# Sums of weight blocks in the retention stage: made by accumulating transfers on GpSimd's queue instead of VectorE, with other signs and another order of the seven block products

## The chip, the cores and the metric

The kernel runs on one core of a Trainium2 chip. The metric is the device time of one execution in microseconds (us), the median of several runs; lower is better. The profile is of one execution, taken by the hardware profiler; its engines are PE (TensorE matmul), PEld (TensorE weight load), DVE (VectorE), ACT (ScalarE), POOL (GpSimd) and SP (SyncE, which here issues the transfers).

## What is computed

The reference is a two-layer decoder trunk over 1024 tokens of width 1024. Layer 0 is retention with four heads; layer 1 is stick-breaking attention. The change lies wholly in layer 0:

```python
u = rms_norm(h, ret_norm_pre[i])
proj = u @ ret_w_in[i]
q, k, v, g = jnp.split(proj, [RET_QK_WIDTH, 2 * RET_QK_WIDTH, 2 * RET_QK_WIDTH + RET_WIDTH], axis=-1)
...
o = retention_chunkwise(q, k, v)
...
o = merge_heads(o).astype(h.dtype) * jax.nn.silu(g)
y = o @ ret_w_out[i]
```

For one head, v is the normed input times a block of 1024 x 512 of the weights, and the gate g is the same input times another such block.

## The kernel before, in words

**Halves and phases.** The tokens are worked in two halves of 512 (t = 0 and 1). For each half, layer 0 goes through its four heads (u = 0 to 3), and a head has three main stages on TensorE: the projection to q and k (`qk`), the projections to v and g (`vg`), and the output projection of the head before (`out`). Of the eight stages for v and g, the first (t = 0, u = 0) is made by plain products (`first_v`, `first_g`); the other seven go through `vg` (lines 453 to 547), which the change rewrites. They start at 147, 251, 338, 461, 567, 675 and 760 us of the profiled span. The second layer runs from about 810 us on and isn't touched.

**Three matmuls for one product.** Every operand is split into a high and a low part (`split`, lines 259 to 266): ScalarE writes the high part (line 262), VectorE subtracts it from the value and so gets the low part (line 263). `mm3` (lines 107 to 112) adds up three matmuls, high x high, high x low and low x high.

**Seven products for eight.** `vg` takes v and g of one head together as one product of 2 x 2 blocks: rows of two blocks of 256 tokens, an inner dimension of two halves of 512, columns v and g. It is done in Winograd's form with seven block products, numbered 1 to 7, for eight. Each is 24 matmuls of 512 columns, in four chunks (`chunk`, line 514); its weights come in two units of 128 x 1024 (i = 0, 1), each of two pieces of 128 x 512 (256 KB). The products 1, 2 and 4 take a block of the weights as it is. Products 5, 6, 3 and 7 take sums and differences of blocks. Product 5 needs the sum of both gate blocks; 6 is that less a block of v; 3 and 7 are made from the one for 6. The running sum is kept in the tile S, one of 128 x 1024 for each i.

**Who makes the weights now.** `left` (lines 460 to 493) loads each piece into a wraw tile (six buffers, line 470), and for products 5, 6, 3 and 7 VectorE adds or subtracts (lines 480, 483, 486, 489); then `split` writes the unit of the matmul's operand, whl (three buffers). The sums of the inputs' blocks on the other side are made once for each half by `sums` (lines 312 to 325).

**What becomes of the products.** The order is 1, 2, 5, 6, 3, 7, 4. PSUM has eight banks, two each with the tags ma, mb, z and o. Product 1 goes to ma and 6 and 7 add to the same banks; 5 goes to mb and 3 adds to it; 2 goes to o; 4 takes mb anew. At the end of products 1, 5, 6 and 7 ScalarE copies the two banks (line 504); VectorE adds copies and banks (line 508) to get v (`vput`, lines 425 to 427, which splits it) and g (`gput`, lines 429 to 432: a sigmoid on ScalarE, a product on VectorE).

**What else lies in the stage.** `begin` (lines 645 to 648) puts the first two or three steps of the retention, `mix` (lines 584 to 643), into the last eight chunks; each takes a bank with tag o (line 607) and sends three small operations to GpSimd (lines 621 to 623), on which ScalarE waits at line 635. In some stages there are also the scores (`scores`, line 567, with a GpSimd select at line 575) or, in the stage from 567 us on, steps that finish the first half (`a_post`: line 693 on VectorE, 694 and 703 on GpSimd, 702 on ScalarE).

**What sets the order.** The source gives an order of steps (`merge`, line 209), which is a priority. The framework makes from it, when the kernel is built, a fixed order for each engine and each queue: an instruction whose inputs and buffers its plan has ready goes into an idle place, ahead of steps that stand before it in the source. On the chip every queue then runs strictly in that order. All transfers of this kernel are issued by SP.

Of the kernel before, what the change touches and what calls it, by code (L numbers as in the profile page):

```python
# [11 lines left out]
F32R = mybir.dt.float32r  # L12
# [19 lines left out]
def trunk(ctx, tc, xT, wts, gains, trig, ident_in, cols, out):  # L32
# [256 lines left out]
    def a_prep(t):  # L289

        X = Ctx()
        X.xh, X.T, X.raw = [None] * 8, [None] * 4, [None] * 4
        X.cos, X.sin = S("tab", [512]), S("tab", [512])

        def tables():
            dma(X.cos[:], trig[0, :, HT * t:HT * t + HT])
            dma(X.sin[:], trig[1, :, HT * t:HT * t + HT])

        tags = ["A"] * 5 + ["AT"] * 3

        def norm(k):
            i, c = k % 4, k // 4
            if t and c == 0:
                X.raw[i] = a_load(t, i, "S")
                if i == 3:
                    tables()
            src = X.raw[i][:, 512 * c:512 * c + 512]
            V.scalar_tensor_tensor(src, src, gcol(G_PRE, k), X.row[:], ALU.mult, ALU.mult)
            x = X.xh[k] = hl("xh")
            split((x[:, 0, :], x[:, 1, :]), src)  # L310

        def sums(i):

            raw = X.raw[i]
            q = [raw[:, 256 * n:256 * n + 256] for n in range(4)]
            X.T[i] = []
            a, b = S("f2", [2, 256]), S("f2", [2, 256])
            V.tensor_tensor(a[:, 0], q[0], q[1], ALU.subtract)
            V.tensor_tensor(a[:, 1], q[2], a[:, 0], ALU.subtract)
            V.tensor_tensor(b[:, 0], q[2], q[0], ALU.subtract)  # L320
            V.tensor_tensor(b[:, 1], q[3], a[:, 1], ALU.subtract)
            for f in (a, b):
                x = S(tags.pop(0), [2, 2, 256], F32R)
                split((x[:, :, 0, :], x[:, :, 1, :]), f[:])
                X.T[i] += [x[:, 0], x[:, 1]]

        if t:
            return X, [f for i in range(4) for f in (lambda i=i: norm(i), lambda i=i: norm(4 + i), lambda i=i: sums(i))]


        first = Ctx()
        first.xh = [None] * 8

        def load(k):
            i, c = k % 4, k // 4
            if c == 0:
                X.raw[i] = S("S" if i < 2 else "ko", [1024])
            src = X.raw[i][:, 512 * c:512 * c + 512]
            dma(src, xT[128 * k:128 * k + 128, 0:HT])
            if k == 0:  # L340
                first.o = S("oT", [4, 2, 512], F32R)
            if k == 4:
                first.o = S("qk", [4, 2, 512], F32R)
            x = first.xh[k] = first.o[:, k % 4]
            split((x[:, 0, :], x[:, 1, :]), src, gcol(G_PRE, k))
            if k == 0:
                first.acc = S("acc", [512])
                A_.activation(first.acc[:], src, AF.Square)
# [60 lines left out]
    class AHead:  # L409
# [16 lines left out]
            x = self.v[tb] = hl("v")  # L426
            split((x[:, 0, :], x[:, 1, :]), src, c)

        def gput(self, tb, src):
            g = self.sg[tb] = S("sg", [512])  # L430
            A_.activation(g[:], src, AF.Sigmoid)
            V.tensor_tensor(g[:], src, g[:], ALU.mult)
# [20 lines left out]
        def vg(self):  # L453


            X, base, h = self.X, self.base, self.h
            self.v, self.sg = [None] * 4, [None] * 4
            box = {"S": [None, None]}

            def left(n, i):  # L460

                w = S("whl", [2, 1024], F32R)
                if n == 5:
                    box["S"][i] = S("S", [1024])
                for c in range(2):
                    cl = slice(512 * c, 512 * c + 512)

                    def load(which, kk):
                        raw = S("wraw", [512])
                        dma(raw[:], wts[base + 4 + 4 * which + kk, :, cl])  # L470
                        return raw[:]

                    s = box["S"][i][:, cl] if box["S"][i] else None
                    if n == 1:
                        src = load(0, i)
                    elif n == 2:
                        src = load(0, 2 + i)
                    elif n == 5:
                        a, b, src = load(1, i), load(1, 2 + i), s
                        V.tensor_tensor(src, a, b, ALU.add)  # L480
                    elif n == 6:
                        a, src = load(0, i), s
                        V.tensor_tensor(src, src, a, ALU.subtract)
                    elif n == 3:
                        src = load(0, 2 + i)
                        V.tensor_tensor(src, src, s, ALU.subtract)
                    elif n == 7:
                        a, src = load(1, 2 + i), s
                        V.tensor_tensor(src, a, src, ALU.subtract)
                    else:  # L490
                        src = load(1, 2 + i)
                    split((w[:, 0, cl], w[:, 1, cl]), src)
                return w

            def right(n, kt, tb):
                tl = slice(128 * tb, 128 * tb + 128)
                if n in (1, 2, 3):
                    x, o = X.xh[kt + (0 if n == 1 else 4)], 0 if n == 3 else 256
                    return [x[:, l, o + 128 * tb:o + 128 * tb + 128] for l in range(2)]
                return [X.T[kt][{5: 0, 6: 1, 7: 2, 4: 3}[n]][:, l, tl] for l in range(2)]  # L500

            def copy(p):
                c = S("f2", [512])
                A_.activation(c[:], p[:], AF.Copy)
                return c

            def plus(c, p):
                V.tensor_tensor(c[:], p[:], c[:], ALU.add)
                return c[:]

            order = [(n, i) for n in (1, 2, 5, 6, 3, 7, 4) for i in range(2)]
            get = ahead(14, lambda at: left(*order[at]))

            def chunk(n, i, kk):
                if kk == 0:
                    at = order.index((n, i))
                    get(at)
                    get(at + 1)
                    box["w"] = get(at)
                    if i == 0:  # L520
# [12 lines left out]
                for tb, p in enumerate(banks):  # L533
                    if n in (1, 5, 6, 7):
                        box[n, tb] = copy(p)
                    if n in (1, 5, 6):
                        pass
                    elif n == 2:
                        self.vput(2 + tb, plus(box[1, tb], p), cc[:, 4 * h + 2 + tb:4 * h + 3 + tb])
                    elif n == 3:  # L540
                        self.vput(tb, plus(box[6, tb], p), cc[:, 4 * h + tb:4 * h + tb + 1])
                    elif n == 7:
# [4 lines left out]
            return Chunks([lambda n=n, i=i, kk=kk: chunk(n, i, kk) for n, i in order for kk in range(2)], lambda: get(0))  # L547
# [612 lines left out]
```

## Time and profile before

| what | value |
|---|---|
| runs: median of 3 (lowest, highest) | 1784.63 us (1782.44 to 1787.44) |
| span of the profiled execution | 1779.2 us |
| instructions | 23669 |
| HBM read, written | 233.93 MB, 56.62 MB |
| busy: PE, DVE, ACT, POOL | 1732.0, 1198.6, 815.1, 290.2 us |

The span goes from the first to the last instruction that the profile has; the median lies 5.4 us above it. A time of an execution includes the start and the end, which the span leaves out. The profile gives the profiled execution no time besides its span, so differences are worked out on the span and added to the median. The page of the profile lists busy times, the span in 40 slices and the costliest groups; the trace behind it can be asked for single stretches.

### The profile page before, as it was taken

The page shows a single profiled execution, that of the slowest core. Times are in us where ns is not written, and L with a number is a line of the kernel's source. Part 1 is how long each engine was busy: PE and PEld are TensorE (multiplying, and loading weights), DVE is VectorE, ACT ScalarE, POOL GpSimd, SP SyncE. Part 2 cuts the span into 40 slices and gives each one's busy share as a digit, 9 for nine tenths or more (in the row PEclk, how much of TensorE's full clock was granted, in tenths as well). Part 3 has the DMA queues.
Part 4 walks back from the last instruction along what each step waited for, and adds up shares of the span by engine and source line. Part 5 has one row for each costly group of instructions (what it writes and reads, how often), then busy time and mean ns, then how long its engine had stood idle before and what let it go on. Part 6 is the DMA issues. An engine that isn't in the chain of part 4 may idle for free.

```text
span 1779.2 us, 23669 instructions
## 1 busy us (share of the span) xinstructions
PE 1732.0 (97%) x8132; PEld 1432.3 (81%) x8132; DVE 1198.6 (67%) x1947; ACT 815.1 (46%) x1526; POOL 290.2 (16%) x377
## 2 busy tenths in 40 slices
PE   8999999999999999999999999999999999999997
PEld 6888788777788788877887888888778888888886
DVE  7756767789766868697485455556677456656675
ACT  6435545455445535364344343444445434444441
POOL 0210412232304320111130100000200010000003
PEclk9999999999999999999999999999999999999999
DMA  5225465557445646275664526345644433522243
GB/s 192 84 101 195 153 236 173 193 179 271 168 143 189 226 144 233 97 258 187 230 222 159 194 95 204 117 151 173 221 135 158 140 131 103 179 94 99 95 137 113
DMA packets 152553, 292.14 MB, mean 164 GB/s; under 512 B 17136, under 2 KB 19312, under 8 KB 152432
## 3 DMA queue, kind: packets, MB, share of 16 engines
q1 hardware_dynamic: 152432, 290.63, 48.2%
q8 instruction: 64, 1.05, 0.2%
q14 instruction: 57, 0.47, 0.1%
HBM read 233.93 MB, written 56.62 MB: 163 GB/s over the span
## 4 chain that ended last, share of the span: by engine, by line
PE 42%; issue 27%; DVE 16%; DMA 7%; POOL 4%; ACT 3%; SPq 1%; POOLq 0%; DVEq 0%; ACTq 0%
PE pma L111 6%; PE pmb L110 6%; PE pmb L111 6%; PE pmb L112 6%; PE pma L112 6%; PE pma L110 6%; DVE whl L263 3%; DMA wraw<-in_wts_dram 3%; PE po L111 2%; PE po L112 2%; PE po L110 2%; DVE sgn L838 1%; POOL small L622 1%; DMA y<-f 1%; DMA S<-in_xT_dram 1%
## 5 line engine op out<-in xcount | busy, mean ns | idle before, releaser
L263 DVE TENSOR_TENSOR whl<-wraw,whl 128x512 fp32r<-128x512 f32 x312 | 220.5, 735 | 67.8 <-ACT whl L262 67.2
L266 DVE SCALAR_TENSOR_TENSOR whl<-wraw,gn,whl 128x256 fp32r<-128x256 f32 (+1 forms) x256 | 153.5, 643 | 127.7 <-ACT whl L265 124.9
L262 ACT ACTIVATE whl<-wraw 128x512 fp32r<-128x512 f32 x312 | 183.5, 624 | 111.5 <-PE pmb L112 52.4
L265 ACT ACTIVATE whl<-wraw,gn 128x256 fp32r<-128x256 f32 (+1 forms) x256 | 143.1, 612 | 166.3 <-PE pmb L112 135.7
L110 PE MATMUL pmb<-xh,whl 128*128 128x512 f32 x384 | 153.1, 399 | 2.8 <-DVE sg L806 2.6
L110 PE MATMUL pma<-xh,whl 128*128 128x512 f32 x384 | 153.3, 399 | 1.2 <-DVE v L263 0.7
L112 PE MATMUL pmb<-xh,whl 128*128 128x512 f32 x384 | 150.3, 391 | 0.0
L112 PE MATMUL pma<-xh,whl 128*128 128x512 f32 x384 | 150.2, 391 | 0.0
L111 PE MATMUL pma<-xh,whl 128*128 128x512 f32 x384 | 149.8, 390 | 0.0
L111 PE MATMUL pmb<-xh,whl 128*128 128x512 f32 x384 | 149.7, 390 | 0.0
L836 POOL TENSOR_SCALAR_AFFINE_SELECT sgn<-sgn 128x128 f32<-128x128 f32 x64 | 24.8, 387 | 692.0 <-ACT sgn L831 580.1
L838 DVE TENSOR_TENSOR_SCAN sgn<-sgn 128x128 f32<-128x128 f32 (+3 forms) x64 | 89.1, 1393 | 45.0 <-POOL sgn L836 45.0
L263 DVE TENSOR_TENSOR AT<-pz,AT 128x512 fp32r<-128x512 f32 (+1 forms) x96 | 53.0, 553 | 72.3 <-ACT AT L262 71.9
L262 ACT ACTIVATE AT<-pz 128x512 fp32r<-128x512 f32 (+1 forms) x96 | 46.7, 487 | 111.5 <-PE pz L868 108.9
L110 PEld LDWEIGHTS pmb<-xh,whl 128*128 128x128 f32 x384 | 72.2, 188 | 18.5 <-DVE sg L806 5.3
L112 PEld LDWEIGHTS pmb<-xh,whl 128*128 128x128 f32 x384 | 72.1, 188 | 15.8
L112 PEld LDWEIGHTS pma<-xh,whl 128*128 128x128 f32 x384 | 72.1, 188 | 15.6
L110 PEld LDWEIGHTS pma<-xh,whl 128*128 128x128 f32 x384 | 72.2, 188 | 15.0 <-DVE v L263 1.1
L111 PEld LDWEIGHTS pmb<-xh,whl 128*128 128x128 f32 x384 | 72.2, 188 | 13.4
L111 PEld LDWEIGHTS pma<-xh,whl 128*128 128x128 f32 x384 | 72.3, 188 | 13.0
L110 PE MATMUL pma<-oT,whl 128*128 128x512 f32 x208 | 82.2, 395 | 0.5 <-DVE small L619 0.5
L111 PE MATMUL pma<-oT,whl 128*128 128x512 f32 x208 | 81.4, 392 | 1.2 <-DVE oT L263 1.2
(321 smaller groups left out, 4507.4 us busy)
## 6 DMA issues: line engine op xcount, KB each, us to landing
wraw<-in_wts_dram SPq DMA_DIRECT2D x624, 256.0 KB, 3.2
y<-f SPq DMA_DIRECT2D x120, 256.0 KB, 3.2
f<-y SPq DMA_DIRECT2D x88, 256.0 KB, 3.8
v<-v SPq DMA_DIRECT2D x16, 512.0 KB, 3.3
vo<-v SPq DMA_DIRECT2D x32, 256.0 KB, 2.9
A<-h SPq DMA_DIRECT2D x12, 512.0 KB, 4.3
st<-ko SPq DMA_DIRECT2D x8, 512.0 KB, 3.9
sg<-in_xT_dram SPq DMA_DIRECT2D x16, 256.0 KB, 2.9
```

Source lines behind the costliest of these rows:

```text
L110: MM(p, lh, rh, start=start, stop=False, **kw)
L111: MM(p, lh, rl, start=False, stop=False, **kw)
L112: MM(p, ll, rh, start=False, stop=stop, **kw)
L262: A_.activation(dst[0], src, AF.Copy)
L263: V.tensor_tensor(dst[1], src, f32(dst[0]), ALU.subtract)
L265: A_.activation(dst[0], src, AF.Copy, scale=scale)
L266: V.scalar_tensor_tensor(dst[1], src, scale, f32(dst[0]), ALU.mult, ALU.subtract)
L622: G.tensor_tensor(r[:], r[:], mhalf[:, 0:1], ALU.pow)
L836: G.affine_select(n[:, dg], n[:, dg], [[-1, 128]], ALU.is_gt, 1.0, base=0, channel_multiplier=1)
L838: V.tensor_tensor_scan(n[:, :W][:, ::-1], n[:, :W][:, ::-1], n[:, :W][:, ::-1], 1.0, ALU.mult, ALU.bypass)
```

## The change

Who adds the weight blocks is changed, and with it the signs and the order.

- A new step `fetch` makes the pieces: a plain transfer from SP brings the first block, and for products 5, 6, 3 and 7 a transfer issued by GpSimd adds a second block to what lies in the tile (`accum_op=ALU.add`). S is summed up in place: gate blocks for 5, a block of v more for 6, the other block of v for 3. Product 7 gets a sum of its own in wraw tiles.
- `left` only splits. The fetch of a unit stands three units ahead of its use in the source, and `begin` fetches three units before the stage starts.
- Since transfers only add, signs move: to the sums of the inputs (`sums`) and to the gate, where `gput` gets the negative of g and multiplies by -1.
- The order is 1, 5, 2, 6, 4, 3, 7. Product 4 uses the banks o, 3 and 7 still add to mb and ma. The copies of products 5 and 4 go into the gate tiles sg, and at the end of product 7 four additions read its two banks, each twice.

```diff
-            V.tensor_tensor(a[:, 0], q[0], q[1], ALU.subtract)
-            V.tensor_tensor(a[:, 1], q[2], a[:, 0], ALU.subtract)
+            V.tensor_tensor(a[:, 0], q[1], q[0], ALU.subtract)
             V.tensor_tensor(b[:, 0], q[2], q[0], ALU.subtract)
-            V.tensor_tensor(b[:, 1], q[3], a[:, 1], ALU.subtract)
+            V.scalar_tensor_tensor(a[:, 1], b[:, 0], -1.0, q[1], ALU.mult, ALU.subtract)
+            V.scalar_tensor_tensor(b[:, 1], a[:, 1], -1.0, q[3], ALU.mult, ALU.subtract)
...
-        def gput(self, tb, src):
+        def gput(self, tb, src, sign=1.0):
+            if sign < 0:
+                f = S("f2", [512])
+                A_.activation(f[:], src, AF.Sigmoid, scale=-1.0)
+                V.scalar_tensor_tensor(src, src, -1.0, f[:], ALU.mult, ALU.mult)
+                return
...
-            def left(n, i):
+            def fetch(n, i):
+                part = {1: (0, i), 2: (0, 2 + i), 4: (1, 2 + i), 5: (1, i), 7: (0, i)}
+                more = {5: (1, 2 + i), 6: (0, i), 3: (0, 2 + i), 7: (1, i)}
                 if n == 5:
                     box["S"][i] = S("S", [1024])
+                src = [box["S"][i][:, 512 * c:512 * c + 512] if n in (5, 6, 3) else S("wraw", [512])[:] for c in range(2)]
+                for c, p in enumerate(src):
+                    if n in part:
+                        which, kk = part[n]
+                        dma(p, wts[base + 4 + 4 * which + kk, :, 512 * c:512 * c + 512])
+                for c, p in enumerate(src):
+                    if n in more:
+                        which, kk = more[n]
+                        G.dma_start(p, wts[base + 4 + 4 * which + kk, :, 512 * c:512 * c + 512], accum_op=ALU.add)
+                return src
+
+            def left(at):
+                src = raw(at)
+                w = S("whl", [2, 1024], F32R)
                 for c in range(2):
...
-                    split((w[:, 0, cl], w[:, 1, cl]), src)
+                    split((w[:, 0, cl], w[:, 1, cl]), src[c])
                 return w
...
-            order = [(n, i) for n in (1, 2, 5, 6, 3, 7, 4) for i in range(2)]
-            get = ahead(14, lambda at: left(*order[at]))
+            order = [(n, i) for n in (1, 5, 2, 6, 4, 3, 7) for i in range(2)]
+            raw = ahead(14, lambda at: fetch(*order[at]))
+            get = ahead(14, left)
...
                     get(at)
                     get(at + 1)
+                    raw(at + 3)
...
-                        first = {1: "ma", 2: "o", 5: "mb", 4: "mb"}.get(n)
+                        first = {1: "ma", 2: "o", 5: "mb", 4: "o"}.get(n)
...
-                    if n in (1, 5, 6, 7):
+                    if n in (1, 6):
                         box[n, tb] = copy(p)
-                    if n in (1, 5, 6):
-                        pass
+                    elif n in (5, 4):
+                        self.sg[tb if n == 5 else 2 + tb] = copy(p, "sg")
...
-                    elif n == 7:
-                        self.gput(tb, plus(box[5, tb], p))
                     else:
-                        self.gput(2 + tb, plus(box[7, tb], p))
+                        plus(self.sg[tb], p)
+                        plus(self.sg[2 + tb], p)
+                if n == 7:
+                    for tb in range(4):
+                        self.gput(tb, self.sg[tb][:], -1.0)
...
+            def begin():
+                for at in range(3):
+                    raw(at)
+                get(0)
```

More of the change, by code (lines that the diff above doesn't have):

```diff
@@ L458, in vg @@
             box = {"S": [None, None]}
-            def left(n, i):
-                w = S("whl", [2, 1024], F32R)
+            def fetch(n, i):
+                part = {1: (0, i), 2: (0, 2 + i), 4: (1, 2 + i), 5: (1, i), 7: (0, i)}
+                more = {5: (1, 2 + i), 6: (0, i), 3: (0, 2 + i), 7: (1, i)}
                 if n == 5:
                     box["S"][i] = S("S", [1024])
+                src = [box["S"][i][:, 512 * c:512 * c + 512] if n in (5, 6, 3) else S("wraw", [512])[:] for c in range(2)]
[8 more added lines that the diff above has]
+                return src
@@ L465, in left @@
+            def left(at):
+                src = raw(at)
+                w = S("whl", [2, 1024], F32R)
                 for c in range(2):
                     cl = slice(512 * c, 512 * c + 512)
[L468 to L486, printed above, removed]
-                    elif n == 7:
[L488 to L491, printed above, removed]
@@ L500, in right, with copy @@
                 return [X.T[kt][{5: 0, 6: 1, 7: 2, 4: 3}[n]][:, l, tl] for l in range(2)]
-            def copy(p):
-                c = S("f2", [512])
+            def copy(p, tag="f2"):
+                c = S(tag, [512])
                 A_.activation(c[:], p[:], AF.Copy)
@@ L541, in chunk @@
                         self.vput(tb, plus(box[6, tb], p), cc[:, 4 * h + tb:4 * h + tb + 1])
-                    elif n == 7:
-                        self.gput(tb, plus(box[5, tb], p))
-                    else:
-                        self.gput(2 + tb, plus(box[7, tb], p))
-            return Chunks([lambda n=n, i=i, kk=kk: chunk(n, i, kk) for n, i in order for kk in range(2)], lambda: get(0))
+                    else:
+                        plus(self.sg[tb], p)
[7 more added lines that the diff above has]
+                get(0)
+            return Chunks([lambda n=n, i=i, kk=kk: chunk(n, i, kk) for n, i in order for kk in range(2)], begin)
         def out(self, y_d, acc=None, tags=None):
```

## The prediction

> **What bounds the kernel now.** First the page's head and the busy times, then the queues.
>
> ```profile
> span 1779.2 us, 23669 instructions
> ...
> PE 1732.0 (97%) x8132; PEld 1432.3 (81%) x8132; DVE 1198.6 (67%) x1947; ACT 815.1 (46%) x1526; POOL 290.2 (16%) x377
> ...
> q1 hardware_dynamic: 152432, 290.63, 48.2%
> ```
>
> TensorE is busy in 97% of the span, but its rows overlap, so the share doesn't say how near it is to its best. The timeline does: rows of the stage that starts at 147 us, the first matmul of product 1 and the first of product 2, 24 matmuls later.
>
> ```profile
> 147.04 0.39 PE L110 MATMUL pma<-whl,xh 128*128 128x512 f32 x1
> 147.27 0.39 PE L111 MATMUL pma<-whl,xh 128*128 128x512 f32 x1
> ...
> 152.48 0.39 PE L110 MATMUL po<-whl,xh 128*128 128x512 f32 x1
> ```
>
> Each row lasts 0.39 us, yet they start every (152.48 - 147.04) / 24 = 0.227 us. That is the pace to compare with; a unit of weights (12 matmuls) is worth 2.72 us, a product 5.44 us. Third, the busy times by stretch, one for each of the seven v and g stages that the change rewrites.
>
> ```profile
> core 0: us, PE busy (x) PEld busy (x) DVE busy (x) ACT busy (x) POOL busy (x), PEclk, DMA share, GB/s
> 147.00:187.20 40.20, 40.20 (x179) 33.26 (x179) 35.54 (x60) 24.89 (x44) 2.88 (x3) 1.00 0.60 201
> 251.40:292.30 40.90, 40.48 (x179) 33.16 (x179) 36.48 (x62) 24.15 (x43) 2.88 (x3) 1.00 0.58 198
> 338.30:386.60 48.30, 47.19 (x217) 38.49 (x216) 39.77 (x68) 29.02 (x53) 14.14 (x7) 0.97 0.66 218
> 460.80:509.20 48.40, 47.48 (x215) 38.81 (x214) 46.89 (x75) 30.22 (x55) 14.90 (x11) 1.00 0.51 175
> 567.40:618.50 51.10, 46.28 (x191) 36.20 (x189) 43.22 (x66) 27.63 (x49) 15.88 (x13) 0.97 0.72 244
> 675.30:719.20 43.90, 43.90 (x199) 36.40 (x198) 38.63 (x65) 26.97 (x47) 2.73 (x5) 1.00 0.59 198
> 760.40:807.50 47.10, 46.63 (x207) 37.82 (x208) 43.52 (x74) 27.93 (x50) 6.38 (x7) 1.00 0.82 271
> sum 319.90, PE 312.17 PEld 254.14 DVE 284.04 ACT 190.80 POOL 59.80; mean PE 44.60 PEld 36.31 DVE 40.58 ACT 27.26 POOL 8.54
> ```
>
> The seven stages take 319.9 us and TensorE idles for 319.90 - 312.17 = 7.7 us of them: nothing in two, 0.4 to 1.1 in four, 4.8 in the one at 567. VectorE is nearly as full, 284 us. So the bound is TensorE at its full pace, and all that faster weights could return is these 7.7 us. The chain of waits shows where the 4.8 are from.
>
> ```profile
> 577.29 4.56 DMA wraw<-in_wts_dram
> ...
> 581.94 0.70 DVE S L483
> ...
> 583.04 4.29 DMA vo<-in_xT_dram
> ...
> 587.47 3.05 POOL vo L694
> ...
> 591.08 0.62 ACT whl L262
> ...
> 591.73 1.36 DVE whl L263
> ...
> 593.77 0.43 PE pma L112
> ...
> 596.33 0.43 PE pma L112
> 596.76 0.28 PE pma L110
> ```
>
> A piece of weights lands late, a load behind it on SP's queue starts late, GpSimd waits for that load, ScalarE waits for GpSimd, and the split behind that is late for TensorE. Then seven matmuls, 593.77 to 596.76, go every 0.43 us: 2.99 us for 7 x 0.227 = 1.59, another 1.4 us, and the stretch's granted clock is 0.97. The Trainium skill ("TensorE: Matmul & The Clock Gate", Part 1: The HAM clock gate) puts half clock down to a whole idle window of about 3.4 us. The chain shows it after waits of which none is that long; by the rule the 1.4 us would not go with the idle, and the forecast would be 1.4 us later.
>
> **The change part by part.** *VectorE's sums go.* Their groups:
>
> ```profile
> L480 DVE TENSOR_TENSOR S<-wraw,wraw 128x512 f32<-128x512 f32 x28 | 20.3, 727 | 28.9 <-DMA wraw<-in_wts_dram 28.8
> L489 DVE TENSOR_TENSOR S<-wraw,S 128x512 f32<-128x512 f32 x28 | 18.9, 681 | 1.2 <-DMA wraw<-in_wts_dram 1.2
> L486 DVE TENSOR_TENSOR wraw<-wraw,S 128x512 f32<-128x512 f32 x28 | 18.9, 689 | 0.0
> L483 DVE TENSOR_TENSOR S<-S,wraw 128x512 f32<-128x512 f32 x28 | 18.5, 689 | 0.6 <-DMA wraw<-in_wts_dram 0.6
> ```
>
> 112 instructions, 76.6 us, 10.9 us for each stage, so VectorE falls from 284 / 7 = 40.6 to about 30 us in a stage of 46. None of it is on TensorE's path by itself; what it can return is the idle. Product 5, now four loads for each unit, waited 28.8 us for them. The two subtractions that become scalar_tensor_tensor in `sums` and the product in `gput` replace instructions of the same size; I take nothing, hidden by the 10.9 us.
>
> *The transfers.* A stage had 32 pieces of 256 KB from SP; it gets 20 from SP and 16 accumulating ones from GpSimd. No row shows an accumulating transfer, nor one issued by GpSimd. The nearest:
>
> ```profile
> wraw<-in_wts_dram SPq DMA_DIRECT2D x624, 256.0 KB, 3.2
> ...
> ko<-st SPq DMA_DIRECT2D x8, 512.0 KB, 6.0
> ```
> ```profile
> L405 POOL TENSOR_TENSOR f<-f,f 128x512 f32<-128x512 f32 x16 | 24.5, 1529 | 0.0
> ```
> ```profile
> 522.10 0.90 SPq L64 DMA_DIRECT2D ko<-st  x2
> ```
> ```profile
> 611.02 0.39 PE L110 MATMUL po<-ko,qk 128*128 128x512 f32 x1
> ```
>
> Issue on GpSimd: between SP's 0.45 us (0.90 / 2) and the 1.5 us that GpSimd needs to compute on such a tile; I take 1.5, as it is GpSimd's own row. Landing: between 3.2 us (the same bytes from HBM) and 6.0 us (twice the bytes); I take 6.0, since the tile is read as well. The pair of one unit: 2 x 1.5 + 6.0 = 9.0 us.
>
> Is there time for it? The last two rows show how far ahead the planned order runs: ko was loaded at 522 as soon as its buffer came free, and used at 611. So the first blocks of product 5 and their sums can be made before the stage. Product 6 adds onto what the split of product 5 has read. whl has three buffers, so that split can start as early as the stage does and takes about 2 us (a 0.62 us row on ScalarE and two of 0.7 on VectorE); product 6 is four units later, 4 x 2.72 = 10.9 us, and its own split must start 2 us before unit 6 (16.3 us). From 2 us to 14.3 us there are 12 us for 9.0. From 6 to 3 it is four units again. Product 7 sums in wraw, and wraw is now used by 16 pieces of a stage, not 32, so its first block lands long before. Estimated effect: nothing is late, and the idle of 7.7 us goes but for some 0.6 us, with the 1.4 us of slow clock behind it: -7.1 - 1.4 = -8.5 us. From below: nothing closes, 0.
>
> *The end of the stage.* Before, the last product (4) left mb, and the next stage began on ma. Now product 7 ends on ma, which the next stage takes first. Rows of the end of the first stage:
>
> ```profile
> 185.57 0.39 PE L112 MATMUL pmb<-whl,AT 128*128 128x512 f32 x1
> ...
> 187.16 0.39 PE L110 MATMUL pma<-xh,whl 128*128 128x512 f32 x1
> ```
> ```profile
> 186.24 1.28 DVE L508 TENSOR_TENSOR f<-pmb,f 128x512 f32<-128x512 f32 x2
> ```
>
> Six matmuls of the retention lie between. Two additions took 1.28 us from 186.24; now there are four, and the banks come free at about 187.5 and 188.8. TensorE wants them at 187.16 and, three matmuls on, 187.84: 0.9 us late. In the three stages of the first half +2.7 us; in the second half twelve matmuls lie there, 1.36 us more, which covers it. Bounds: 0, if the additions start as the bank ends, and seven times four exposed additions, 7 x 2.5 = 17.5 us.
>
> *The order* 1, 5, 2, 6, 4, 3, 7 gives v's first block at the end of product 3, just ahead of the retention step that reads it, where product 7 lay between before. The planner can put matmuls of product 7 first; I take nothing (bounds 0 and 3 x 2 us).
>
> Sum: -8.5 + 2.7 = **-5.8 us**, 1773.4 us of span. The median is 5.4 us above the span; -5.8 from it gives 1784.6 - 5.8 = **1778.8 us**.
>
> **The rivals.** *GpSimd's queue runs late and ScalarE with it (slower).* GpSimd works in order, and so does ScalarE behind it. The waits before, the first over the span, the others in the stage at 567:
>
> ```profile
> ACT sgn L635 <- POOL small L623: 98.1, 31, 6.3
> ```
> ```profile
> POOL vo L694 <- DMA vo<-in_xT_dram: 16.2, 3, 12.5
> ACT vo L702 <- POOL vo L694: 8.2, 3, 3.2
> ```
>
> An accumulating transfer stands on that queue until its first block has landed or the split has read S; behind it wait the selects of the scores, the small operations for line 635 and the additions of line 694, and behind those ScalarE's splits. ScalarE already waits 3.2 us each time, and the case of 567 shows the price once the cover of three whl buffers is gone: 4.8 + 1.4 = 6.2 us. It decides once GpSimd runs some 5 us (two units) behind its plan. At a quarter to a half of 6.2 us in each of the other six stages: +9 to +19, 1794 to 1803 us. For it: 16 transfers of 1.5 us add 24 us of issue where GpSimd had 8.5 us of work. Against: 32 of 46 us.
>
> *The DMA engines fill up (slower).* 48.2% of 1779.2 us for 290.63 MB is 0.77 us of all engines for each 256 KB. If an accumulating piece costs k of these, a stage gets (4 + 16(k - 1)) x 0.77 us more, less the eight transfers of product 5 that move ahead of it. At k = 2 no stage is full. At k = 3 the stage at 760 (share 0.82) is over by 7 us and that at 567 by 1; at k = 4 all are, by 59 us together. So it decides from k = 3, and would give 1787 to 1838, about 1811 in the middle. The Trainium skill ("DMA: Bandwidth & Descriptors", Queues, rings and completion order) says that each engine takes turns between the queues that have work, packet by packet: GpSimd's queue would then take half of a full engine from SP's loads. All transfers here are on q1, so no row shows it; by the rule it would come earlier.
>
> *The change does nothing for TensorE.* The weights come earlier, but the idle hangs on other loads, as vo above: 1784 us, between 1780 and 1789.
>
> *The banks ma hold up every stage fully:* 1784.6 - 8.5 + 17.5 = 1794 us.
>
> **How the numbers follow.** A difference of about 0.3%, 5.4 us, is what a measurement of this kernel can tell from none. The forecast has 0.46: its own range is 1775 (no bank wait, all idle gone) to 1783 (half of the idle gone), 0.39 of it faster by over 0.3% (below 1779.3) and 0.07 the same. Nothing for TensorE: 0.17, of it 0.15 the same, 0.01 faster, 0.01 slower. GpSimd late: 0.21, the engines full 0.13, the banks 0.03, all slower. Faster 0.40, same 0.22, slower 0.38. The range from 1774 to 1804 takes in all but the upper part of the full engines (0.1) and the tails.
>
> **What would show it.** Right: the groups of lines 480 to 489 are gone; in the seven stages TensorE's idle sums to under 3 us; matmuls start every 0.227 us from the first product on; accumulating transfers land within 6 us; the only new wait is that of `pma` on line 508's successor at a stage's end, under 1 us. Wrong: waits of whl's split for S or wraw over 2 us at products 6 or 3 (the pair takes over 12 us); the wait of line 635 for line 623 well over 100 us; a DMA share at 1 in a stage; granted clocks below 0.97.

## The result, and the profile after

Over four runs the changed kernel took 1815.61 us (1814.35 to 1822.12), and the kernel before 1785.41 us beside it: a ratio of 1.0177 [1.0157, 1.0196]. It is 30 us slower, and above the range of the prediction. The profiled execution has a span of 1814.9 us against 1779.2, 35.7 us more; the time of every run on record is 1.7 to 2.0 us above its span, so the profiled execution of the kernel before took about 1781 us, 4.5 us under the median, and some 5 of the 35.7 us are only that.

First the page of the changed kernel: head, busy times, the two queues of transfers (packets, MB, share of 16 engines) and the issues (count, size, median us from issue to landing).

```profile
span 1814.9 us, 23719 instructions
...
PE 1748.3 (96%) x8132; PEld 1440.1 (79%) x8132; DVE 1137.5 (63%) x1835; ACT 813.7 (45%) x1526; POOL 366.1 (20%) x489
...
q1 hardware_dynamic: 140336, 268.60, 44.4%
q0 software_dynamic: 16128, 29.37, 9.7%
...
wraw<-in_wts_dram SPq DMA_DIRECT2D x512, 256.0 KB, 3.4
...
S<-in_wts_dram POOLq DMA_DIRECT2D x84, 256.0 KB, 6.8
...
S<-in_wts_dram SPq DMA_DIRECT2D x28, 256.0 KB, 5.6
wraw<-in_wts_dram POOLq DMA_DIRECT2D x28, 256.0 KB, 5.7
```

VectorE lost the 112 instructions, but only 61 us of busy time (1198.6 to 1137.5) where the groups had 76.6. Two rows stand out. The 112 accumulating transfers lie on a queue of their own, q0, and take 9.7% of the engines for 29.37 MB, 0.330% for each MB; the plain ones on q1 take 44.4% for 268.60 MB, 0.165%. Per byte an accumulating transfer costs **2.0 times** the engine time of a plain one. And S takes 6.8 us to land where 3.2 was the median of a piece before; the plain first blocks in S take 5.6 too. The 3.4 us of wraw by SP look unchanged, but they are the median over the whole kernel. Worked out from issue and landing of those that SP issues inside the seven stages, the median is 5.9 us (115 pieces), where it was 3.5 before (226 pieces): plain loads, on a queue of their own, land late there as well.

The stretches, one for each of the seven v and g stages, show where the time went. Columns as before: length, busy times, granted clock, DMA share, GB/s.

```profile
147.00:192.60 45.60, 43.09 (x179) 33.92 (x178) 25.73 (x42) 25.43 (x45) 15.74 (x19) 0.96 0.85 203
258.20:304.10 45.90, 43.09 (x179) 34.05 (x179) 26.84 (x44) 24.97 (x44) 15.50 (x19) 0.96 0.86 200
351.30:402.50 51.20, 47.58 (x219) 39.01 (x218) 30.39 (x51) 28.50 (x52) 14.47 (x19) 0.97 0.76 187
476.60:526.40 49.80, 48.55 (x215) 38.54 (x213) 33.93 (x54) 26.92 (x49) 21.50 (x27) 1.00 0.79 185
585.20:643.50 58.30, 48.28 (x191) 37.41 (x190) 37.52 (x49) 27.46 (x51) 31.83 (x32) 0.94 0.94 240
700.30:747.00 46.70, 44.70 (x199) 35.92 (x197) 26.43 (x44) 23.27 (x41) 16.80 (x20) 1.00 0.87 203
790.50:842.60 52.10, 48.07 (x209) 39.57 (x209) 39.25 (x62) 29.56 (x54) 14.49 (x19) 0.95 0.82 215
sum 349.60, PE 323.38 PEld 258.43 DVE 220.10 ACT 186.12 POOL 130.34; mean PE 46.20 PEld 36.92 DVE 31.44 ACT 26.59 POOL 18.62
```

The kernel before, with the stages between the same points of the work (two of the prediction's stages begin or end up to 0.4 us otherwise):

```profile
sum 320.30, PE 312.64 PEld 254.51 DVE 284.44 ACT 190.93 POOL 59.80; mean PE 44.66 PEld 36.36 DVE 40.63 ACT 27.28 POOL 8.54
```

Of the 35.7 us, 29.3 lie in the seven stages (349.60 - 320.30). TensorE's idle grew from 7.7 to 26.2 us (+18.5). Its busy time grew by 10.7 us with the same matmuls. Most of that is the half clock: the granted clock is 0.94 to 0.97 in five stages, and the share that it lacks times the length of the stage comes to 11.3 us, where it came to 3.0 before (two stages at 0.97). The other 2.4 us of busy time weren't followed up. 6.4 us of the span lie outside the seven stages; of these, 4.1 are there without any addition too (e2 below), and their cause is open.

The DMA share is what moved with it: 0.51 to 0.82 before, 0.76 to 0.94 now. Inside the first stage it is higher where the sums of product 3 are due. The same two stretches in the changed kernel, and in e2, where the transfers of GpSimd are plain copies (the share counts the whole time of every packet that starts in the stretch, so it can pass 1):

```profile
163.00:178.00 15.00, 14.69 (x65) 11.61 (x63) 7.22 (x11) 6.63 (x11) 6.96 (x8) 1.00 0.92 209
178.00:190.00 12.00, 9.89 (x34) 7.36 (x35) 8.50 (x15) 6.85 (x13) 4.36 (x6) 0.86 1.02 267
```
```profile
163.00:178.00 15.00, 15.00 (x68) 12.42 (x67) 9.73 (x15) 9.22 (x17) 4.51 (x9) 1.00 0.84 282
178.00:190.00 12.00, 11.93 (x53) 9.59 (x52) 10.97 (x19) 8.10 (x15) 2.57 (x5) 1.00 0.75 263
```

With additions TensorE loses 2.1 us in the second stretch, at a clock of 0.86 and a DMA share of 1.02; without them it loses next to nothing (0.1 us), at 0.75.

The waits of the changed kernel (engine, tile, line <- releaser: sum in us, times, longest in us):

```profile
ACT sgn L640 <- POOL small L628: 98.6, 31, 6.3
...
ACT whl L262 <- DMA S<-in_wts_dram: 24.8, 15, 4.6
...
POOL S L479 <- issue: 23.0, 17, 4.0
...
POOL wraw L479 <- issue: 19.9, 12, 3.4
...
PE pma L110 <- DVE sg L504: 2.6, 4, 1.8
```

Three rows are of use. ScalarE, which splits the weights, now waits 24.8 us for S itself to land. GpSimd stands 42.9 us at its accumulating transfers for a reason that the profile calls issue: no tile and no engine holds it. And the wait behind GpSimd's small operations, the first rival's sign, is as before (98.1 then, 98.6 now).

Nor is it weights of these products alone that come late. In the stage at 585 the chain of waits runs through another load, and at the end of the stage at 700 through the next weights, whose median had been 3.2 us:

```profile
593.38 5.96 DMA vo<-y
...
599.46 0.06 DVE vo L698
...
600.13 3.60 DVE whl L263 x4
```
```profile
735.12 8.23 DMA wraw<-in_wts_dram
```

### The profile page after: what moved, and what is told of

Its sections match the earlier page's. It is cut to its first block, busy times and chain, and to the rows that moved or that the text cites. A ratio compares the mean times of both kernels' runs of the same rounds, so it can differ in the third digit from the quotient of the medians.

```text
span 1814.9 us, 23719 instructions
## 1 busy us (share of the span) xinstructions
PE 1748.3 (96%) x8132; PEld 1440.1 (79%) x8132; DVE 1137.5 (63%) x1835; ACT 813.7 (45%) x1526; POOL 366.1 (20%) x489
## 3 DMA queue, kind: packets, MB, share of 16 engines
q1 hardware_dynamic: 140336, 268.60, 44.4%
q0 software_dynamic: 16128, 29.37, 9.7%
## 4 chain that ended last, share of the span: by engine, by line
PE 34%; issue 23%; DVE 7%; DMA 6%; POOL 3%; ACT 1%; SPq 0%; POOLq 0%; DVEq 0%; ACTq 0%
PE pma L110 5%; PE pma L111 5%; PE pma L112 5%; PE pmb L110 4%; PE pmb L112 4%; PE pmb L111 4%; DMA wraw<-in_wts_dram 2%; PE po L111 2%; PE po L112 2%; PE po L110 2%; DMA S<-in_wts_dram 1%; DVE sgn L843 1%; DVE whl L263 1%; DMA A<-h 1%; DVE A L844 1%
## 5 line engine op out<-in xcount | busy, mean ns | idle before, releaser
L263 DVE TENSOR_TENSOR whl<-S,whl 128x512 fp32r<-128x512 f32 x84 | 61.8, 765 | 72.8 <-ACT whl L262 72.8
L479 POOL DMA_DIRECT2D S<-in_wts_dram x84 | 77.3, 993 | 121.5 <-DVE whl L263 46.9
L263 DVE TENSOR_TENSOR AT<-pz,AT 128x512 fp32r<-128x512 f32 (+1 forms) x96 | 53.1, 554 | 71.7 <-ACT AT L262 71.4
L110 PEld LDWEIGHTS pmb<-xh,whl 128*128 128x128 f32 x384 | 72.4, 189 | 19.9 <-DVE sg L811 5.3
L112 PEld LDWEIGHTS pmb<-xh,whl 128*128 128x128 f32 x384 | 72.2, 188 | 15.9
L111 PE MATMUL pma<-oT,whl 128*128 128x512 f32 x208 | 81.3, 391 | 1.8 <-DVE oT L263 1.8
```

The source lines that it names most:

```text
L110: MM(p, lh, rh, start=start, stop=False, **kw)
L111: MM(p, lh, rl, start=False, stop=False, **kw)
L112: MM(p, ll, rh, start=False, stop=stop, **kw)
L263: V.tensor_tensor(dst[1], src, f32(dst[0]), ALU.subtract)
L479: G.dma_start(p, wts[base + 4 + 4 * which + kk, :, 512 * c:512 * c + 512], accum_op=ALU.add)
```

## The experiments

Three theories at the start. **A:** only a few accumulating transfers fit in flight, so GpSimd waits for room before it can issue the next, and the sums come late. **B:** an accumulating piece takes the engines twice as long, and everything that lands beside it lands later. **C:** the other order of products and the other place of the first retention step.

What bears on A: from issue and landing of the 112 transfers, never more than three are under way at once, and 71 were issued as the third. The Trainium skill ("DMA: Bandwidth & Descriptors", SWDGE vs HWDGE vs iDMA) says that the descriptors of GpSimd's transfers stand in rings in a reserved part of SBUF. The size of that part is set where the program is made, at 1024 here, so it can be changed alone.

**e1: the room doubled.** Every queue keeps its instructions and their order.

```diff
-    nc = bacc.Bacc("TRN2", target_bir_lowering=False, num_devices=1, dynamic_dma_scratch_size=1024)
+    nc = bacc.Bacc("TRN2", target_bir_lowering=False, num_devices=1, dynamic_dma_scratch_size=2048)
```

> The changed kernel with twice the space for GpSimd's transfer descriptors (2048 for 1024); every queue has the same instructions in the same order. Theory A (only three accumulating transfers fit in flight, and the fourth waits on GpSimd until the first has landed): the gaps between issues go, the sums of product 3 land some 5 us earlier, and 10 to 20 us of the 30 come back, about 1798. Theory B (the accumulating transfers take the DMA engines twice as long and every load lands later): no change beyond 3 us, about 1814. Theory C (the order puts the retention's first step right behind product 3, which makes its v): no change, 1814.

1807.46 us, 1.0128 [1.0113, 1.0143]: 8 us of the 30 come back, between the 1798 expected of A and the 1814 of B. Its waits:

```profile
POOL wraw L479 <- issue: 7.3, 3, 4.6
...
POOL S L479 <- issue: 0.5, 1, 0.5
```

The wait for room is nearly gone (42.9 to 7.8 us), up to six transfers are under way, and 22 us stay. Even the 8 us aren't all the room's: of the 8.6 us between the two spans (1814.9 and 1806.3), 4.0 lie in the seven stages (349.60 - 345.60) and 2.8 behind the last of them, mostly in the second layer, where the two kernels are the same. The timeline shows why the rest stays. GpSimd's sums in S for product 3 in the first stage, the changed kernel and then e1:

```profile
170.20 0.89 POOL L479 DMA_DIRECT2D S<-in_wts_dram  x1 [1.37 <-issue]
171.90 0.88 POOL L479 DMA_DIRECT2D S<-in_wts_dram  x1 [0.82 <-DVE whl L263]
```
```profile
165.49 2.75 POOL L479 DMA_DIRECT2D S<-in_wts_dram  x2
```

The first is issued 4.7 us earlier (170.20 to 165.49), the second 5.9 us (171.90 to 166.04 in the trace). The splits on ScalarE that wait for them, again the changed kernel and e1:

```profile
176.53 0.63 ACT L262 ACTIVATE whl<-S 128x512 fp32r<-128x512 f32 x1 [4.28 <-DMA S<-in_wts_dram]
...
178.02 0.63 ACT L262 ACTIVATE whl<-S 128x512 fp32r<-128x512 f32 x1 [0.86 <-DMA S<-in_wts_dram]
```
```profile
176.15 0.63 ACT L262 ACTIVATE whl<-S 128x512 fp32r<-128x512 f32 x1 [3.51 <-DMA S<-in_wts_dram]
...
178.09 0.63 ACT L262 ACTIVATE whl<-S 128x512 fp32r<-128x512 f32 x1 [1.31 <-DMA S<-in_wts_dram]
```

They start at nearly the same time. By the trace the two sums land at 176.4 and 178.0 us in the changed kernel, 6.2 and 6.1 us after their issue, and at 176.0 and 178.1 us in e1, 10.6 and 12.0 us after it. The transfers had more room and were no sooner done; that it was engine time that they lacked is what e2 tests.

**e2: the same transfers, without adding.** GpSimd's 112 transfers are plain copies, at the same places and in the same order on every queue; the additions of the second blocks are left out.

```diff
-                        G.dma_start(p, wts[base + 4 + 4 * which + kk, :, 512 * c:512 * c + 512], accum_op=ALU.add)
+                        G.dma_start(p, wts[base + 4 + 4 * which + kk, :, 512 * c:512 * c + 512])
```

> The changed kernel with GpSimd's transfers as plain copies; it leaves out the additions of the weight blocks (the second block overwrites the first). Same bytes from HBM, same queues, waits and order. Theory B: packets on GpSimd's queue take 0.09 us and not 0.19, the DMA share of the seven stages falls from 0.76 to 0.94 to some 0.65 to 0.8, loads land as before the change, and 15 to 25 us come back, about 1795. Theory A: plain copies need fewer descriptors, so part of the same gain; the difference from the run with twice the space is what the engines' time costs. Theory C: no more than 5 us come back, 1811.

1786.70 us, 1.0004 [0.9994, 1.0014]: all 30 us come back, more than the 15 to 25 expected of B, with the same bytes, queues and order. From its page:

```profile
q0 software_dynamic: 8960, 29.37, 4.9%
...
S<-in_wts_dram POOLq DMA_DIRECT2D x84, 256.0 KB, 4.2
...
S<-in_wts_dram SPq DMA_DIRECT2D x28, 256.0 KB, 3.9
```

4.9% for 29.37 MB is the plain price, 0.167 per MB. Most of the difference is in the number of packets, 8960 for 16128; one packet takes 0.156 us here and 0.175 with the addition (the share times 16 engines times the span, by the number of packets), so the fall from 0.19 to 0.09 for each packet that was expected is not how it comes about. S by GpSimd lands in 4.2 us, not 6.8, and S by SP in 3.9, not 5.6, though nothing was changed about SP's transfers; the pieces of wraw that SP issues inside the stages land in 3.7 us, not 5.9. Between the spans of these two kernels of one order lie 29.7 us (1814.9 and 1785.2), and 27.4 of them in the seven stages (349.60 and 322.20).

Two other things change with the addition. A plain copy takes less room (up to six are under way here at 1024), which e1 and e5 look at alone. And GpSimd issues it in 0.55 us for up to 0.99, which no run has alone; the sums that e1 issued 4.7 and 5.9 us earlier and that landed no sooner speak against it.

What e2 shows as well: with VectorE relieved and no addition on the engines, the kernel is no faster than before. (It still differs from the kernel before by the order of the products and by 28 pieces more to load, so what the relief is worth alone isn't shown.) Its seven stages:

```profile
sum 322.20, PE 313.97 PEld 255.43 DVE 222.65 ACT 191.40 POOL 92.84; mean PE 44.85 PEld 36.49 DVE 31.81 ACT 27.34 POOL 13.26
```

VectorE has 62 us less to do in them (284.44 to 222.65), and TensorE idles 8.2 us (322.20 - 313.97), where it was 7.7.

**e3: the changed order, with VectorE's sums.** SP loads the second block into wraw, and VectorE adds it.

```diff
-                        G.dma_start(p, wts[base + 4 + 4 * which + kk, :, 512 * c:512 * c + 512], accum_op=ALU.add)
+                        b = S("wraw", [512])
+                        dma(b[:], wts[base + 4 + 4 * which + kk, :, 512 * c:512 * c + 512])
+                        V.tensor_tensor(p, p, b[:], ALU.add)
```

> The changed kernel's order, signs, banks and copies, but all loads from SP and the sums made by VectorE in place. If the accumulating transfers are the loss (A or B): about the time before, 1780 to 1790. Theory C (the order is the loss): 1800 to 1815, with the same wait of the retention's first step for v.

1804.19 us, 1.0114 [1.0098, 1.0129]. That is in the range expected of C (1800 to 1815) and well above that of A and B (1780 to 1790). But the wait that C named, the first retention step's for v, is 2.7 us here where the changed kernel has 4.8, and e2 has the changed order of products too and loses nothing. The edit also changes the planned order on every engine and queue. The wait that it has and the others lack:

```profile
DVE S L481 <- DMA wraw<-in_wts_dram: 41.5, 26, 4.7
```

Six wraw tiles carry 32 pieces of a stage, as before the change, but now they are taken three units ahead. Of the 23.9 us by which its span is longer than that of the kernel before, 14.8 lie outside the seven stages. In one place the trace shows how: VectorE waits 2.9 us, until 322.3, for a piece of the next stage, the split of oT stands behind that sum on its queue, and TensorE waits 5.4 us for it, where it waited 1.8 before. That all of the loss is of this kind was not tried by itself and stays open.

**e4: the first retention step later**, the second part of C. The edit also changes the planned order of TensorE, VectorE and ScalarE; the queues of GpSimd and SP keep theirs.

```diff
-                       [([], 0, 0) if 0 < u < 3 else (H.scores(), 3, 15), (H.begin(), 20, 0), (more, 4, 8)])
+                       [([], 0, 0) if 0 < u < 3 else (H.scores(), 3, 15), (H.begin(), 24 if t == 0 else 20, 0), (more, 4, 8)])
```

> The changed kernel with the retention's first step of the first half put one product later (from chunk 24 on, not 20), so that product 7 lies between it and the v that it reads. Theory C: the waits of 2 to 4 us at the first step go in the three stages of the first half, with the half-clock matmuls behind them, 8 to 15 us back, about 1804. Theories A and B: 0 to 4 us back, 1812 to 1816.

1819.07 us, 1.0187 [1.0170, 1.0205], no better, where C was to bring back 8 to 15 us. With e2, which has the order and the place of the step and loses nothing, C falls. The wait at a stage's end grows with the edit, from 2.6 us:

```profile
PE pma L110 <- DVE sg L504: 4.8, 4, 2.5
```

**e5: the room halved, without adding.** As e2 (the additions are left out), with 512 for 1024; the same order. If waiting for room costs time by itself, it must show here.

```diff
-    nc = bacc.Bacc("TRN2", target_bir_lowering=False, num_devices=1, dynamic_dma_scratch_size=1024)
+    nc = bacc.Bacc("TRN2", target_bir_lowering=False, num_devices=1, dynamic_dma_scratch_size=512)
```

> The run with plain copies from GpSimd (the additions of the weight blocks are left out) with half the space for its descriptors (512 for 1024), same order on every queue. If the space alone holds the queue back (theory A), at most three or so plain copies are in flight, and the time goes from 1787 towards 1795 to 1800. If the engines' time is the loss and a short queue hurts only beside it (theory B): 1786 to 1790.

1786.90 us, 1.0012 [1.0001, 1.0023]. Its waits:

```profile
POOL S L479 <- issue: 12.3, 8, 3.1
...
POOL wraw L479 <- issue: 12.0, 9, 3.9
```

GpSimd waits 24 us for room, with three transfers at most under way, and the ratio is 1.0012 for e2's 1.0004, with intervals that overlap. So waiting for room costs little by itself. Beside busy engines it is 4 to 8 us of the 30 (e1).

**e6: the kernel before, with accumulating transfers for product 5 alone**, 28 of them.

```diff
-                        a, b, src = load(1, i), load(1, 2 + i), s
-                        V.tensor_tensor(src, a, b, ALU.add)
+                        src = s
+                        dma(src, wts[base + 4 + 4 + i, :, cl])
+                        G.dma_start(src, wts[base + 4 + 4 + 2 + i, :, cl], accum_op=ALU.add)
```

> The kernel before with one part of the change: the sum of product 5 made in S by a plain and an accumulating transfer, ahead of the stage; order, signs and VectorE's other sums as before. 28 accumulating transfers, so a quarter of the engines' extra time. Theory B: the share of the stages rises by 0.02 to 0.07 only, product 5 no longer waits for four loads, and the time is 1777 to 1785. If accumulating transfers hurt by GpSimd's in-order queue, few or many: 1790 to 1800.

1783.02 us, 0.9995 [0.9983, 1.0007]: no difference that can be told, and within the 1777 to 1785 expected of B.

**e7: the same with VectorE's addition.** The first block of product 5 still goes straight into S.

```diff
-                        a, b, src = load(1, i), load(1, 2 + i), s
-                        V.tensor_tensor(src, a, b, ALU.add)
+                        src = s
+                        dma(src, wts[base + 4 + 4 + i, :, cl])
+                        b = load(1, 2 + i)
+                        V.tensor_tensor(src, src, b, ALU.add)
```

> The kernel before, with the first block of product 5 loaded straight into S ahead of the stage and the second added by VectorE; no transfer from GpSimd. If what can be gained is the wait of product 5 for its wraw buffers: 1778 to 1783, the same as or better than with the accumulating transfer. If VectorE's time for the sum is what matters: no gain, 1784 to 1787.

1776.66 us, 0.9968 [0.9955, 0.9981], a little faster than the kernel before and below the range expected (1778 to 1783). Its seven stages:

```profile
sum 316.50, PE 311.00 PEld 254.52 DVE 283.22 ACT 190.52 POOL 47.83; mean PE 44.43 PEld 36.36 DVE 40.46 ACT 27.22 POOL 6.83
```

VectorE works as much as before (283.22 us), and TensorE idles 5.5 us for 7.7. The gain comes without VectorE's relief. That it comes of the load that goes straight to S, one wraw tile less for each piece, is likely but not shown: e6 has that load too, beside its additions, and gains nothing that can be told.

**e8: product 7 on VectorE**, 84 accumulating transfers left, room 2048.

```diff
-                        G.dma_start(p, wts[base + 4 + 4 * which + kk, :, 512 * c:512 * c + 512], accum_op=ALU.add)
+                        if n in (7,):
+                            b = S("wraw", [512])
+                            dma(b[:], wts[base + 4 + 4 * which + kk, :, 512 * c:512 * c + 512])
+                            V.tensor_tensor(p, p, b[:], ALU.add)
+                        else:
+                            G.dma_start(p, wts[base + 4 + 4 * which + kk, :, 512 * c:512 * c + 512], accum_op=ALU.add)
```

> The changed kernel with twice the descriptor space and product 7's sums made by VectorE from a load on SP: 84 accumulating transfers, not 112. Theory B: the extra engine time falls by a quarter, 4 to 8 us back from 1807.5, about 1801. If the planned order of the changed kernel is the loss, and not the transfers' number: 1805 to 1812.

1818.86 us, 1.0207 [1.0190, 1.0224]: a miss, above both ranges (about 1801, and 1805 to 1812). The planned order changed on all queues with this edit, as in e3, and it says nothing clean of the dose. Its loss is of another kind:

```profile
PE pma L110 <- DVE sg L509: 15.4, 4, 4.4
```

At the ends of four stages TensorE waits up to 4.4 us for the banks of product 7, 15.4 us in all where the changed kernel has 2.6. That is what the prediction's rival of the banks ma had in mind (17.5 us at most), and the changed kernel is spared it. From here on only kernels with the order of the changed kernel are compared.

**e9 and e10: half of the additions.** B has two forms: B1, the load on the engines makes everything late; B2, only the chain through S is late, where 6 and 3 add onto what 5 made. In e9 only the transfers for 5 and 7 add (the additions of 6 and 3 are left out), in e10 only those for 6 and 3 (the additions of 5 and 7 are left out). Room 2048, the same order.

```diff
-                        G.dma_start(p, wts[base + 4 + 4 * which + kk, :, 512 * c:512 * c + 512], accum_op=ALU.add)
+                        G.dma_start(p, wts[base + 4 + 4 * which + kk, :, 512 * c:512 * c + 512], **(dict(accum_op=ALU.add) if n in (5, 7) else {}))
```

> The changed kernel with twice the descriptor space and the same order on every queue; products 5 and 7 accumulate, the transfers for 6 and 3 are plain copies (their additions are left out). Half the accumulating transfers, and those with the most time ahead of their use. If every load suffers from the engines' time (B1): half of the 20 us between 1807.5 and 1786.7, about 1797, the same as its counterpart. If the loss is the own landing time of the sums in the chain 5, 6, 3 (B2): 1787 to 1790.

> The counterpart: products 6 and 3 accumulate, the transfers for 5 and 7 are plain copies (their additions are left out). B1: about 1797 as well. B2: 1804 to 1808.

1794.1 us, 1.0058 [1.0043, 1.0073], and 1792.72 us, 1.0044 [1.0029, 1.0058]. Their q0 rows, e9 first:

```profile
q0 software_dynamic: 12544, 29.37, 7.4%
```
```profile
q0 software_dynamic: 12544, 29.37, 7.6%
```

Both stand halfway between the plain 4.9 and the accumulating 9.7 or so. B2 had e9 at 1787 to 1790 us and e10 at 1804 to 1808; they are 1.4 us apart, the other way about, with intervals that overlap, so B2 falls. B1 had both at about 1797, 3 to 4 us too high. The pieces of wraw that SP issues inside the stages stand between too: 4.3 and 5.0 us to land, where e2 has 3.7 and e1 5.8. The dose, by runs with one order:

| kernel | additions | mean DMA share of the stages | us | ratio |
|---|---|---|---|---|
| e2 | 0 | 0.68 | 1786.70 | 1.0004 |
| e9, e10 | 56 | 0.77, 0.81 | 1794.1, 1792.72 | 1.0058, 1.0044 |
| e1 | 112, room 2048 | 0.85 | 1807.46 | 1.0128 |
| changed kernel | 112, room 1024 | 0.84 | 1815.61 | 1.0177 |

By the ratios the first 56 cost 7 to 10 us and the next 56 12 to 15, each give or take about 3: the price seems to rise as the engines fill. But the mean share of one stage doesn't give its loss. The sixth stage of e1 loses nothing at 0.90 (44.0 us for 43.9), and the third of e9 is 4.4 us longer than before at 0.62 (53.1 for 48.7): it matters which load is late.

## Why the prediction was wrong

**The step that failed first: "At k = 2 no stage is full."** k is 2.0, as the rows of q0 and q1 show. The working took "the eight transfers of product 5 that move ahead" off each stage; but in five of the seven stages the next head's eight are issued near the end of the same stage, so nothing is to be taken off; only the third and the last have none of them. Without that, the first stage has 0.60 x 40.2 + 20 x 0.77 = 39.5 us of engine time in what became 45.6 us, a share of 0.87; measured 0.85. Even so the corrected sum puts only one of the five over its length, the one at 567, by 1 us (0.72 x 51.1 + 20 x 0.77 = 52.2 us). So the larger fault is the other half of the sentence: a mean share below 1 was taken for free. The transfers of a stage aren't spread evenly: 0.92 and 1.02 stand in its second half, and there the loads land late. The rival "The DMA engines fill up" had the right resource, but it was said to decide "from k = 3" and so had a chance of 0.13. That its 1811 us "in the middle" are near the 1815.6 measured is luck: they stand between k = 3 and k = 4, and count only what runs over a full stage.

**The landing.** "I take 6.0" was the upper bound, the same tile with twice the bytes. Measured: 6.8 us in S, 5.7 in wraw. The bound came from rows with the engines as they were before, and the change itself filled them; nor did the working let SP's own transfers land later, which is where the seven stages lose as well (S by SP 5.6 against 3.9 in e2). The 12 us of room for a pair stood against 9.0 us, and as a sum that held (two issues of 0.99 and a landing of 6.8 are 8.8 us). What it left out is that several pairs are under way at once: the second sum of product 3 was issued at 171.90 us after a wait for room, which the prediction didn't have at all, and in e1, where it was issued at 166.04, it took 12.0 us to land.

**The gain.** "The idle of 7.7 us goes" failed without any addition as well: e2 frees VectorE, with the order of the changed kernel, and TensorE's idle is 8.2 us. The prediction had said that none of VectorE's sums is on TensorE's path by itself, and that the idle is that of late loads; it should have stopped there. The case without gain, 1784 us between 1780 and 1789, takes in what e2 measures.

**Right.** TensorE bounds the stages at 0.227 us a matmul. Issue on GpSimd lay within the bounds of 0.45 and 1.5 us, under the 1.5 that was taken. The groups of line 479, the changed kernel and then e2 (busy, mean ns of one, idle before and its releasers):

```profile
L479 POOL DMA_DIRECT2D S<-in_wts_dram x84 | 77.3, 993 | 121.5 <-DVE whl L263 46.9 <-DMA S<-in_wts_dram 33.8 <-issue 23.0
L479 POOL DMA_DIRECT2D wraw<-in_wts_dram x28 | 24.7, 893 | 69.9 <-DVE whl L263 27.3 <-DMA wraw<-in_wts_dram 21.8 <-issue 19.9
```
```profile
L479 POOL DMA_DIRECT2D S<-in_wts_dram x84 | 46.5, 554 | 97.7 <-DVE whl L263 50.0 <-DMA S<-in_wts_dram 33.2 <-ACT A L262 5.9
```

The adding ones took 0.99 and 0.89 us each. The cost of the first retention step "nothing" holds for the order: the bank of that step waits 0.6 us in e2, which has the same order. In the changed kernel it is 4.8 us in three waits, behind a late product 3. The waits of the two, the changed kernel first:

```profile
PE po L110 <- ACT v L265: 4.8, 3, 2.1
```
```profile
PE po L110 <- ACT v L265: 0.6, 1, 0.6
```

The first rival, ScalarE late behind GpSimd's small operations, didn't come: 98.6 us for 98.1.

**Right by luck.** The wait for the bank at a stage's end was forecast at 2.7 us, 0.9 in each stage of the first half and none in the second. Its row has 2.6, but all four waits are in the second half, at 526 to 528 and at 747 to 748 us, the longest of 1.8; the first half has none, and e2 has none at all.

**The half clock.** The prediction set the Trainium skill's rule ("TensorE: Matmul & The Clock Gate", Part 1: The HAM clock gate), a whole idle window of about 3.4 us, against a chain that had none. The runs stand with the chain: between 178 and 190 us TensorE has 2.1 us of idle in all and the clock is 0.86; the clock's record has half clock for 3.41 us from 184.80 us on, right behind a wait of 2.1 us.

Open: the 4.1 us outside the stages that e2 has too, most of the loss of e3, what GpSimd's longer issue costs by itself, and which part of e7's edit brings its 0.32%.

## What to carry to other kernels

Price a transfer that adds at twice a plain one on all the engines, and lay it on the stretch where it runs, with what the neighbouring stages push into it, not on the stage's mean: here 7 to 10 us were lost at mean shares of 0.77 to 0.81, 22 at 0.85, and 30 at 0.84 with less room. Look at the landing of loads inside the stage, since a median over the whole kernel hid it here (3.4 us for 5.9). Don't count on a gain from work taken off an engine that isn't late for anyone: here 62 us less on VectorE came with none. When a plan orders the queues, compare only kernels whose order is the same: leaving out the addition in the same transfer (e2) settled in one run what e3 and e8 could not. And look where a wait lies before calling a forecast of its sum right.

## What the runs showed of the hardware

- A transfer of GpSimd that adds takes 2.0 times the engine time of a plain one per byte (0.330 against 0.165% per MB) and, in these stages, 6.8 us to land 256 KB where the plain one took 4.2. Beside them, plain loads of 256 KB issued by SP inside these stages took 5.9 us to land, and 3.7 where the additions were left out.
- Transfers of GpSimd under way at once: adding, three at a size of 1024 and up to six at 2048; plain, three at 512 and up to six at 1024. By these numbers an adding one takes about twice the room; it also has more packets, 16128 on q0 for 8960.
- Issuing costs GpSimd 0.89 to 0.99 us for one that adds, and 0.55 for a plain one.
- In the first stage of the changed kernel half clock was granted to TensorE for 3.41 us behind an idle stretch of 2.1 us.
